# An encoder block's first stage as one explicit list of small operations

## The chip, the cores and the metric

The kernel runs on one core of one Trainium2 chip. The core has five engines with instruction queues of their own: TensorE (PE; its weight loads are shown as PEld), VectorE (DVE), ScalarE (ACT), GpSimd (POOL) and SyncE (SP), which here only issues DMA transfers. Each queue runs in order; engines wait for each other through semaphores. The metric is the device time of one execution in microseconds (us), the median of three runs.

## What is computed

One bidirectional encoder layer on 1024 tokens of width 1024, all in float32 at the interface:

```python
u = rms_norm(x, norm1_g)
q, k, v, cb, cc, ch, ga, gb = split(u @ w_in)        # 512 x 6, then 1024 x 2 columns
q, k = rms_norm(q per head, q_norm_g), rms_norm(k per head, k_norm_g)   # 8 heads of 64
y_a = neighbourhood_attention(q, k, v, rpb) @ w_attn_branch
y_b = (cb * conv3(cc * ch)) @ w_conv_branch
x = x + (sigmoid(ga) * y_a + sigmoid(gb) * y_b) @ w_o
x = x + relu(rms_norm(x, norm2_g) @ w_mlp_in) ** 2 @ w_mlp_out
```

The change concerns the part that comes first: the norm of the rows of x, the product for v, sums of normed rows that a later stage uses for the gates ga and gb (the gate forms), and the first four of eight row blocks of the product for q.

## The kernel before, in words

**Precision.** Every matmul operand is held as two float16 halves, a `hi` (the value, scaled by a power of two and rounded) and a `lo` (the remainder). A product is three passes: hi·hi, hi·lo and lo·hi (`PASSES`). ScalarE makes a `hi` with an activation that copies and scales; VectorE makes the `lo` with `scalar_tensor_tensor` (value times scale, minus `hi`). The power of two comes from a bound over all 128 partitions: a per-partition bound is written into one column of the bfloat16 tile `ones`, one matmul of the all-ones block with that column sums it over the partitions in a bank of PSUM (128x1 output), and VectorE reads it back and works out exponents with a handful of 128x1 instructions (`all_sum`, `pow2`, `pow2_half`).

**Row blocks.** The 1024 tokens are 8 blocks of 128 rows. `load_x(b)` brings block b into `xt`. `norm` squares it on ScalarE with an accumulated sum, works out the reciprocal root of the mean in a few 128x1 VectorE steps and a ScalarE square root (`rstd`), and makes `hi` and `lo` in `u16`, which has room for four blocks. Blocks 0, 1 and 2 are transposed into `uT` by TensorE (`ln_trans`: eight 128x128 transposes for each half into a bank of PSUM, copied out by ScalarE and by VectorE); blocks 3 to 7 by a DMA transpose that SP issues (`ln_turn`).

**V.** The weights of v come in two column halves of 256. For row blocks 0 to 2, each half is a group of its own of 24 matmuls of 256 columns (8 slices of the inner dimension by 3 passes); for blocks 3 to 7 both halves are one group of 24 matmuls of 512 columns (`v_unit`). A part of the weights' `lo` is made on POOL, in two steps.

**Gate forms.** `sforms` runs for four pairs of row blocks (n, n + 4): ScalarE scales both blocks of `xt`, POOL makes four sums and differences of 512 columns, ScalarE rounds them to `hi` (128x2048), VectorE makes the `lo`, and SP stores both in the DRAM tile `gs`.

**Q and K.** For each of the 8 row blocks a group of 24 matmuls of 512 columns for q, then 8 more for k. The result is evicted and processed by `qk_vec`: ScalarE copies and squares, VectorE sums per head, the reciprocal root follows, VectorE scales, ScalarE makes `hi`, VectorE makes `lo` into one of two `q16` buffers, and `finish_qk` has SP transpose it by DMA into `QD` or `KD`. `QD` lies where `xt` was, so its first transpose waits for the last reader of `xt`.

**What sets the order.** Instructions are issued by the program order of Python generators. Foreground generators (`fg`: for example `qk_vec`, `sforms`) go on by `step()`, background ones (`bg`: the preparation of weight chunks, `Chunk.prep`, pushed chunk by chunk) by `tick()`; `unit` issues one group of matmuls and then so many steps and ticks. A generator can hold itself back with `apart(mark, n)` until the counter `units[0]` has reached a value; `flush` sets `forced` and runs the background to its end. For the chunks Q, K and C, `Chunk.prep` squares each weight tile on ScalarE, adds the sums up on VectorE, waits, sums over the partitions with the ones matmul, waits for one more unit, reads back, and scales. The waits are these lines:

```python
                yield from apart(units[0], 2 if self.kind in "QC" else 3)
                yield from all_sum(c, b, bank(self.bank) if self.bank else anybank(), 1e-36)
```

The chunk K is pushed in front of Q's first unit, and the last Q unit is followed by `flush()`. Weight tiles come through a pool of five raw buffers; a tile's load is issued when an earlier tile has been split (`load_upto(done[0] + 5)`).

Of the kernel before, what the change touches and what calls it, by code (L numbers as in the profile page):

```python
# [28 lines left out]
def plan():  # L29


    def block(w, groups, per=2, tiles=8, first=0):
        return [(w, first + k, per, groups) for k in range(0, tiles, per)]

    p = [(("V", j), block("w_in", [(1024 + 256 * j, 256)], 4)) for j in range(2)]
    p += [(("Q", 0), block("w_in", [(0, 512)])), (("K", 0), block("w_in", [(512, 512)]))]
    p += [(("C", j), block("w_in", [(c + 128 * j, 128) for c in (2048, 2560, 1536)])) for j in range(4)]
    branch = lambda j: [((k, j), block(w, [(256 * j, 256)], 4, 4)) for k, w in (("A", "w_a"), ("B", "w_b"))]
    for n in range(8):
        p.append((("S" if n else "G", n), block("w_in", [(3072 + 128 * n, 128), (4096 + 128 * n, 128)], 4)))  # L40
# [30 lines left out]
def encoder_block(ctx: ExitStack, tc: tile.TileContext, x, weights, cols, gqk, rel, masks, out):  # L71
# [16 lines left out]
    def bank16(tag):  # L88
        return psum.tile([128, 1024], F16, name="ps16_" + tag, tag=tag, bufs=banks[tag])
# [23 lines left out]
    def tmp(n=1):  # L113
        return cols_of("tmp", n)
# [267 lines left out]
    def load_x(b):  # L382
        SP.dma_start(xt[:, b], x[b * 128:(b + 1) * 128, :])
# [18 lines left out]
    idi = w1p.tile([128, 128], I32, name="idi", bufs=1)  # L402
    ident = w1p.tile([128, 128], F16, name="ident", bufs=1)
# [43 lines left out]
    def norm(xin, sq, u, y):  # L447

        ss = tmp()
        A.activation(sq, xin, AF.Square, accum_out=sc[:, ss])  # L450
        yield
        yield from rstd(ss, D, y, 9)
        A.activation(u[:, 0], xin, AF.Copy, scale=sc[:, y])
        yield
        V.scalar_tensor_tensor(u[:, 1], xin, sc[:, y], u[:, 0], op0=OP.mult, op1=OP.subtract)

    def ln_trans(u16, b, dst):
        for s in range(2):
            pt = bank16("o")
            for k in range(8):  # L460
                T.transpose(pt[:, k * 128:(k + 1) * 128], u16[:, s, k * 128:(k + 1) * 128], ident)
            o = dst[:, s, :, b * 128:(b + 1) * 128]
            i = pt.rearrange("p (k t) -> p k t", k=8)
            if s == 0:
                A.activation(o, i, AF.Copy)
            else:
                V.tensor_copy(o, i)

    def ln_turn(u16, b, dst):
        SP.dma_start_transpose(dst[:, :, :, b * 128:(b + 1) * 128].rearrange("p s k t -> p (s k) t"),  # L470
                               u16.rearrange("p s k -> p (s k)"))
# [19 lines left out]
    sgq, isgq = keep(), keep()  # L491
    sq = w1p.tile([128, D], F32, name="sq", bufs=1)
    ys = keep(8)
    ln = [norm(xt[:, b], sq, u16[:, b % 4], at(ys, b)) for b in range(8)]
    GS = dram.tile([128, 4, 4, 2, 512], F16, name="gs")

    turned, formed = [0], [0]
    SFORM = (6, 8, 10, 12)

    def sforms():  # L500

        for n, start in enumerate(SFORM):
            yield from apart(start, 0)
            assert turned[0] >= n + 5
            z = []
            for b in (n, n + 4):
                A.activation(xt[:, b], xt[:, b], AF.Copy, scale=sc[:, at(ys, b)])
                z += [xt[:, b, :512], xt[:, b, 512:]]
            f = wqk.tile([128, 4, 512], F32, name="sform", bufs=1)
            v = wqk.tile([128, 4, 2, 512], F16, name="s16", bufs=2)  # L510
            for o, a, b, op in ((2, z[0], z[2], OP.subtract), (0, z[2], z[3], OP.subtract),
                                (1, f[:, 0], z[0], OP.subtract), (3, z[1], f[:, 1], OP.add)):
                G.tensor_tensor(f[:, o], a, b, op=op)
            yield from apart(start, 2)
            A.activation(v[:, :, 0], f, AF.Copy)
            yield
            V.tensor_tensor(v[:, :, 1], f, v[:, :, 0], op=OP.subtract)
            fg.append(sform_store(n, v))

    def sform_store(n, v):  # L520
        yield from apart(units[0], 1)
        SP.dma_start(GS[:, n], v)
        formed[0] = n + 1

    def ln_step(b, n=1):
        for _ in range(n):
            advance(ln[b])
# [7 lines left out]
    def v_unit(b, j, steps, ticks):  # L535
        ps = bank("ds"[b % 2])
        n, c = (512, 0) if j is None else (256, 256 * j)

        def post():
            hi, lo = (VT[:, b, s, c:c + n] for s in range(2))  # L540
            A.activation(hi, ps[:, :n], AF.Copy, scale=2.0 ** -20)
            V.scalar_tensor_tensor(lo, ps[:, :n], 2.0 ** -20, hi, op0=OP.mult, op1=OP.subtract)
        w = vhome[0] if j is None else vhome[0][:, j]
        unit(group(ps[:, :n], [(UT[:, sa, k, b * 128:(b + 1) * 128], w[..., sw, k * 256:(k + 1) * 256])
                               for k in range(8) for sa, sw in PASSES]), post, steps, ticks)

    push(cV[0])
    ln_step(0, 2)
    tick()
    ln_step(0, 5)  # L550
    ln_step(1)
    tick(3)
    ln_step(0)
    ln_step(1)
    tick(4)
    ln_trans(u16[:, 0], 0, UT)
    flush()
    ln_step(1, 5)
    ln_step(1)
    ln_step(2, 2)  # L560
    push(cV[1])
    tick(1)
    v_unit(0, 0, 0, 0)
    ln_step(2, 4)
    ln_trans(u16[:, 1], 1, UT)
    ln_step(2, 1)
    tick(3)
    ln_step(2)
    tick(4)
    ln_step(3, 2)  # L570
    ln_trans(u16[:, 2], 2, UT)
    ln_step(3, 4)
    fg.append(qk_gain())
    fg.append(sforms())
    V.tensor_reduce(sc[:, gm2], sc[:, g1], axis=AX, op=OP.max, apply_absolute_value=True)
    mul(gm2, gm2, gm2)
    for p in range(11):
        if p == 3:
            flush()
            push(cQ)  # L580
        if 0 < p < 6:
            v_unit(p % 3, p // 3, 1, 2)
        elif p:
            v_unit(p - 3, None, 2, 4)
        for q in (p,) if p < 6 else (2 * p - 6, 2 * p - 5):
            c = q // 2 + 3
            if c < 8 and q % 2 == 0:
                ln_step(c, 2)
                ln_turn(u16[:, c % 4], c, UT)
                turned[0] = c + 1  # L590
            if c < 7:
                ln_step(c + 1, 3)
    settle()
    flush()
# [41 lines left out]
    def finish_qk(n):  # L636
# [3 lines left out]
        dst = QD.rearrange("p a e w t -> p (a e w) t") if kind == "q" else KD  # L640
        SP.dma_start_transpose(dst[:, :, b * 128:(b + 1) * 128], q16.pop(n)[0].rearrange("p h w r d -> p (h w r d)"))

    for n, (kind, b) in enumerate(todo):
        ch = cQ if kind == "q" else cK
        if b == 0:
            push(cK if kind == "q" else cConv[0])
        ps = bank("do"[n % 2])
        q16[n] = []

        def post(ps=ps, kind=kind, n=n, ch=ch):  # L650
            fg.append(qk_vec(ps, ch.inv, kind, q16[n]))
        unit(tok_mms(ps, actU, b, ch, 8, 512, 0), post, 4, 3)
        if n == 3:
            forced[0] = True
            while formed[0] < 4:
# [1218 lines left out]
```

## Time and profile before

| what | us |
|---|---|
| median of 3 runs | 1238.45 (1238.36 to 1238.69) |
| profiled execution | 1236.77 |
| its span | 1235.0 |
| TensorE busy in the span | 1196.9 (97%) |
| VectorE / ScalarE / POOL busy | 936.9 / 765.9 / 430.3 |
| start of the first matmul | 9.49 |
| start of the first K group | 114.30 |

How to read the profile: the page gives busy times and shares. The timeline has one row for each instruction or for a few alike in a row: its start and its length in us, engine, line of the kernel, operation, output tile, input tiles, shape, count; in brackets the idle time of the engine before it and the instruction that ended it. The length of a matmul row contains a modelled end; from one group's start to the next is the better measure. All vector and scalar instructions have the line of the recording helper, L66, so they are told apart by their tiles: `u` is a row block's halves, `w_v` V's weight halves, `w_ws` those of Q, K and the later chunks, `s` a gate form's halves, `q` a Q block's halves, `sc` the small columns. The windows view has for each stretch the busy time of PE, PEld, DVE, ACT and POOL with instruction counts, then the clock granted to TensorE as a share, the DMA share and GB/s. The groups view has the count, the sum of busy us and the mean in ns. The DMA view has KB and the median us from issue to landing.

### The profile page before, as it was taken

What the parts mean: (1) busy time and instruction counts of PE and PEld (TensorE: products, weight loads), DVE (VectorE), ACT (ScalarE), POOL (GpSimd) and SP (SyncE); (2) the same over time, 40 slices, a digit from 0 to 9 for tenths busy, and PEclk for the clock granted to TensorE, in tenths of its full rate; (3) what the DMA queues carried; (4) which work ended last, traced back from release to release, by engine and by line L of the source; (5) the groups of instructions that cost most, each with busy time, mean ns of one, the idle gap of its engine ahead of it and who ended that gap; (6) DMA issues with size and microseconds to landing.
All of it is one profiled execution on the core that took longest, in us unless ns stands there. A gap on an engine that the chain in (4) does not pass through costs nothing.

```text
span 1235.0 us, 16691 instructions
## 1 busy us (share of the span) xinstructions
PE 1196.9 (97%) x6102; PEld 576.9 (47%) x6102; DVE 936.9 (76%) x1747; ACT 765.9 (62%) x1185; POOL 430.3 (35%) x289
## 2 busy tenths in 40 slices
PE   5989999999899999999999999999999999999998
PEld 3534445555444444444458444444444444444444
DVE  6668778888558786877878664555547999999997
ACT  6777667768644454535768777777775763646430
POOL 2440003232212111101003466655648373463562
PEclk8999999999899999999999999999999999999999
DMA  6558455565761211216096653454474844435202
GB/s 258 107 200 178 103 118 112 116 153 105 131 154 34 69 52 51 69 35 255 18 174 152 205 170 137 162 187 142 140 290 162 313 155 159 168 116 222 103 35 103
DMA packets 170867, 173.34 MB, mean 140 GB/s; under 512 B 131488, under 2 KB 132000, under 8 KB 166688
## 3 DMA queue, kind: packets, MB, share of 16 engines
q1 hardware_dynamic: 170784, 172.27, 47.2%
q8 instruction: 48, 0.79, 0.3%
q14 instruction: 35, 0.29, 0.1%
HBM read 102.51 MB, written 37.75 MB: 114 GB/s over the span
## 4 chain that ended last, share of the span: by engine, by line
PE 40%; DVE 6%; ACT 2%; issue 2%; DMA 1%; DVEq 0%; ACTq 0%
PE ps_d L207 16%; PE ps_s L207 14%; PE ps_o L207 10%; DVE as L66 1%; DVE ops L66 1%; DVE w L66 1%; DVE form L66 1%; ACT as L66 1%; DVE v L66 1%; DMA u2T<-v 1%; DMA u2x<-v 1%; ACT ops L66 1%; DVE x L66 0%; DVE sc L66 0%; ACT u2x L66 0%
## 5 line engine op out<-in xcount | busy, mean ns | idle before, releaser
L207 PEld LDWEIGHTS <-ops 128*128 128x128 f16 x1356 | 132.4, 98 | 159.9 <-issue 2.7
L207 PEld LDWEIGHTS <-w 128*128 128x128 f16 x1368 | 132.8, 98 | 143.5 <-issue 3.8
L924 PE MATMUL ps_d<-uT,w_ws 128*128 128x512 f16 x576 | 136.7, 382 | 0.0
L207 PE MATMUL ps_s<-ops 128*128 128x512 f16 (+1 forms) x528 | 118.3, 374 | 0.0
L207 PE MATMUL ps_d<-ops 128*128 128x512 f16 x504 | 115.6, 379 | 0.0
L66 ACT ACTIVATE ops<-hf,sc 128x2048 f16<-128x2048 f32 x26 | 52.0, 1999 | 94.0 <-PE ps_d L207 52.7
L207 PE MATMUL ps_d<-u2T,w 128*128 128x512 f16 (+1 forms) x504 | 110.3, 371 | 0.0
L1074 POOL TENSOR_TENSOR tsum<-raw 128x512 f32<-128x512 f32 x28 | 46.6, 1677 | 148.1 <-ACT raw L66 148.1
L207 PEld LDWEIGHTS <-uT 128*128 128x128 f16 x648 | 64.9, 101 | 70.5 <-issue 5.6
L1278 POOL TENSOR_TENSOR as<-as 128x512 f32<-128x512 f32 x56 | 76.7, 1370 | 41.4 <-ACT as L66 38.1
L207 PEld LDWEIGHTS <-w_s 128*128 128x128 f16 x588 | 56.9, 98 | 68.6 <-DVE w_s L66 0.6
L924 PEld LDWEIGHTS <-w_ws 128*128 128x128 f16 x576 | 56.1, 98 | 59.7 <-issue 2.0
L207 PE MATMUL ps_s<-u2x,w 128*128 128x512 f16 (+1 forms) x348 | 78.6, 375 | 0.0
L207 PE MATMUL ps_o<-ops 128*128 128x512 f16 x324 | 74.3, 379 | 2.4 <-DVE as L66 2.4
L66 DVE SCALAR_TENSOR_TENSOR ops<-hf,sc,ops 128x2048 f16<-128x2048 f32 x26 | 71.7, 2759 | 5.7 <-ACT ops L66 5.7
L66 ACT ACTIVATE raw<-raw,sc 128x256 f32<-128x256 f32 x172 | 71.1, 494 | 6.7 <-DMA raw<-in_weights 6.7
L66 DVE TENSOR_TENSOR as<-ps_s,as 128x512 f32<-128x512 f32 (+1 forms) x38 | 23.4, 616 | 58.5 <-ACT as L66 57.9
L66 DVE TENSOR_SCALAR sc<-sc 128x1 int32<-128x1 int32 (+3 forms) x380 | 57.6, 167 | 12.9 <-ACT sq L66 4.3
L1074 POOL TENSOR_TENSOR gsum<-raw 128x512 f32<-128x512 f32 x14 | 18.5, 1340 | 136.8 <-issue 52.3
L66 ACT ACTIVATE w<-raw,sc 128x512 f16<-128x512 f32 (+1 forms) x29 | 25.4, 920 | 50.8 <-DVE sc L66 50.8
L66 ACT ACTIVATE sz<-sz,sc 128x384 f32<-128x384 f32 (+1 forms) x64 | 37.2, 581 | 26.8 <-DVE sc L66 26.6
L66 DVE SCALAR_TENSOR_TENSOR w_ws<-raw,sc,w_ws 128x512 f16<-128x512 f32 (+2 forms) x72 | 48.5, 712 | 6.7 <-ACT w_ws L66 6.7
(261 smaller groups left out, 2548.6 us busy)
## 6 DMA issues: line engine op xcount, KB each, us to landing
raw<-in_weights SPq DMA_DIRECT2D x89, 512.0 KB, 5.5
hs<-as SPq DMA_DIRECT2D x16, 1792.0 KB, 8.7
hf<-hs SPq DMA_DIRECT2D x26, 1024.0 KB, 6.7
w2x<-in_weights SPq DMA_DIRECT2D x16, 512.0 KB, 8.3
raw<-in_weights SPq DMA_DIRECT2D x16, 384.0 KB, 3.7
xt<-in_x SPq DMA_DIRECT2D x8, 512.0 KB, 9.8
gs<-s SPq DMA_DIRECT2D x4, 1024.0 KB, 6.4
x<-in_x SPq DMA_DIRECT2D x8, 512.0 KB, 10.0
```

Source lines behind the costliest of these rows:

```text
L66: return f(out, *a, **kw)
L207: T.matmul(ps, l, r, start=a, stop=b)
L924: T.matmul(ps, l, r, start=a, stop=b)
L1074: G.tensor_tensor(t[:, o], a, b, op=OP.add)
L1278: sub.tensor_tensor(z[o], z[a], z[b], op=op)
```

## The change

The generators `norm`, `ln_trans`, `ln_turn`, `sforms`, `sform_store` and `v_unit`, and the loop that stepped them, are removed. In their place stands one string, `BEGIN`, of words such as `V.1.0.hh.0`; a table `DO` maps a word's first part to a small function, and a loop calls them in the string's order. So each engine's queue is the string's order, projected on that engine. From the fifth Q unit on the old loop goes on, with four ticks instead of three beside each of the last four Q units.

The words: `sq`, `ts`, `sqrt`, `y` are the steps of a row block's norm; `hi` (on POOL for seven blocks, on ScalarE for block 5), `lo`; `Th`, `Tl` the TensorE transposes of blocks 0 to 2, `ch`, `cl` their copies; `turn` a DMA transpose; `tr`, `col`, `one`, `scal` the scale of V's weights, `whi`, `wlo` their halves by 512 columns; `V.b.h.pass.k` four matmuls of one pass; `vh`, `vl` the eviction of V; `zs`, `sp`, `sh`, `sl`, `st` a gate form's scaling, POOL sums, `hi`, `lo` and store; `qs` to `qlo` the same for Q's weights, `Q.b.r` six matmuls, `qc` to `ql` the steps of `qk_vec` for the block, `ldQ`, `ldK` a weight load, and `ks` one square of K's weights (the first also pushes the chunk K).

```diff
+BEGIN = """
+    gm2 sq.0 ts.0 tr.0 sqrt.0 y.0 tr.1 col.0 hi.0.P sq.1 lo.0 Th.0 sq.2 ts.1 one.0 sqrt.1 scal.0 ts.2 ch.0.A
+    Tl.0 sqrt.2 whi.0.1 y.1 whi.0.0 V.0.0.hh.0 whi.1.1 whi.1.0 y.2 hi.1.P Th.1 cl.0.V lo.1 Tl.1 wlo.0.1.P
...
+    hi.6.P V.1.1.hl.1 V.3..hl.0 ldQ.3 V.3..hl.1 vh.3. turn.4 vl.2.0 hi.7.P V.4..hh.0 V.4..hh.1 zs.5
+    V.4..lh.0 qs.1 sl.0 st.0 V.4..lh.1 vh.2.1 vh.1.1 lo.6 qs.0 V.4..hl.0 turn.5 V.4..hl.1 V.5..hh.0
+    V.5..hh.1 V.5..lh.0 turn.6 lo.7 gain qs.3 vl.0.1 vl.1.1 vl.2.1 V.5..lh.1 V.5..hl.0 V.5..hl.1 turn.7 qs.2
...
+    vh.6. zs.7 sh.2 sl.2 st.2 V.7..hl.0 V.7..hl.1 Q.0.0 Q.0.1 Q.0.2 Q.0.3 ldK.0 vl.4. zs.3 Q.1.0 ldK.2 vl.6.
+    Q.1.1 Q.1.2 qc.0 ks.0 Q.1.3 ks.1 Q.2.0 ldK.3 Q.2.1 Q.2.2 Q.2.3 qr.0 qc.1 qr.1 qc.2 qq.0 vh.7. vl.7. qy.0
+    sp.3 ks.2 ks.3 qh.0 Q.3.0 ql.0 sh.3 Q.3.1 sl.3 st.3 Q.3.2 Q.3.3
+"""
...
     load_x(1)
+    load_x(2)
     load_upto(4)
-    load_x(2)
     load_x(3)
+    load_x(4)
+    load_x(5)
     load_upto(5)
+    load_x(6)
+    load_x(7)
...
-    for b in range(4, 8):
-        load_x(b)
...
+    def rows_hi(b, e):
+        o, y = u16[:, b % 4, 0], sc[:, at(ys, b)]
+        if e:
+            G.tensor_scalar(o, xt[:, b], y, 1.0, op0=OP.mult, op1=OP.mult)
+        else:
+            A.activation(o, xt[:, b], AF.Copy, scale=y)
...
+    def v_mms(b, h, kind, kh):
+        g = vgroups.index((b, h))
+        if (kind, kh) == ("hh", 0):
+            vbank[g] = bank("ds"[g % 2])
+        ps = vbank[g][:, :512 if h is None else 256]
+        sa, sw = {"hh": (0, 0), "lh": (1, 0), "hl": (0, 1)}[kind]
+        for k in range(4 * kh, 4 * kh + 4):
+            w = vw[:, :, sw, k * 256:(k + 1) * 256] if h is None else vw[:, h, sw, k * 256:(k + 1) * 256]
+            T.matmul(ps, UT[:, sa, k, b * 128:(b + 1) * 128], w, start=(kind, k) == ("hh", 0),
+                     stop=(kind, k) == ("hl", 7))
...
+    def q_mms(b, r):
+        if r == 0:
+            vbank["q", b] = bank("ds"[(len(vgroups) + b) % 2])
+        for k in (2 * r, 2 * r + 1):
+            for n, (sa, sw) in enumerate(PASSES):
+                T.matmul(vbank["q", b], UT[:, sa, k, b * 128:(b + 1) * 128], cQ.parts[:, sw, 512 * k:512 * k + 512],
+                         start=(k, n) == (0, 0), stop=(k, n) == (7, 2))
+        units[0] += r == 3
...
+          "st": lambda n: SP.dma_start(GS[:, n], sf[n, 1]), "ks": lambda r: (r == 0 and push(cK), tick(1))}
+
+    for word in BEGIN.split():
+        name, *args = word.split(".")
+        DO[name](*[None if name in ("V", "vh", "vl") and a == "" else int(a) if a.isdigit() else a for a in args])
+
+    for b in range(4):
+        q_vec(b, 0)
+        fg.append(qv[b])
...
-        if b == 0:
-            push(cK if kind == "q" else cConv[0])
-        ps = bank("do"[n % 2])
-        q16[n] = []
-
-        def post(ps=ps, kind=kind, n=n, ch=ch):
-            fg.append(qk_vec(ps, ch.inv, kind, q16[n]))
-        unit(tok_mms(ps, actU, b, ch, 8, 512, 0), post, 4, 3)
-        if n == 3:
-            forced[0] = True
-            while formed[0] < 4:
-                step()
-            forced[0] = False
+        if kind == "k" and b == 0:
+            push(cConv[0])
+        if n == 4:
...
-        if n >= 3:
+        if n >= 4:
+            ps = bank("do"[n % 2])
+            q16[n] = []
+
+            def post(ps=ps, kind=kind, n=n, ch=ch):
+                fg.append(qk_vec(ps, ch.inv, kind, q16[n]))
+            unit(tok_mms(ps, actU, b, ch, 8, 512, 0), post, 4, 4 if n < 8 else 3)
             finish_qk(n - 3)
```

More of the change, by code (lines that the diff above doesn't have):

```diff
@@ L445, in pow2_half @@
         yield
[L447 to L471, printed above, removed]
     PASSES = ((0, 0), (0, 1), (1, 0))
@@ L533, in qk_gain @@
         yield from gain(g, 11, sgq, isgq)
[L535 to L594, printed above, removed]
     def bias_load(p):
@@ new lines, in rows_hi, with rows_lo, rows_trans @@
+    def rows_hi(b, e):
[4 more added lines that the diff above has]
+            A.activation(o, xt[:, b], AF.Copy, scale=y)
+    def rows_lo(b):
+        V.scalar_tensor_tensor(u16[:, b % 4, 1], xt[:, b], sc[:, at(ys, b)], u16[:, b % 4, 0],
+                               op0=OP.mult, op1=OP.subtract)
+    pt = {}
+    def rows_trans(b, s):
+        pt[b, s] = bank16("o")
+        for k in range(8):
+            T.transpose(pt[b, s][:, k * 128:(k + 1) * 128], u16[:, b % 4, s, k * 128:(k + 1) * 128], ident)
@@ new lines, in v_col, with w_sum, v_scale @@
+    def v_col(h):
+        m = tmp()
+        mul(g1, rv[h], rv[h])
+        V.tensor_reduce(sc[:, m], sc[:, rv[h]], axis=AX, op=OP.max, apply_absolute_value=True)
+        wcol[h] = ones_col()
+        V.tensor_copy(wcol[h], sc[:, m])
+    def w_sum(h):
+        wbank[h] = bank("o")
+        T.matmul(wbank[h][:, 0:1], ones[:, 0:128], wcol[h], start=True, stop=True)
+    def v_scale(h):
+        b, s = tmp(), tmp()
+        cV[h].inv = keep()
+        V.tensor_scalar(sc[:, b], wbank[h][:, 0:1], 1e-30, None, op0=OP.max)
+        for _ in pow2(b, 14, s, cV[h].inv, False, more=9):
+            pass
+        V.tensor_scalar(sc[:, rv[h]], sc[:, g1], sc[:, s], None, op0=OP.mult)
@@ new lines, in v_out, with q_square @@
+    def v_out(b, h, s):
+        ps = vbank[vgroups.index((b, h))][:, :512 if h is None else 256]
+        hi, lo = (VT[:, b, i, (h or 0) * 256:(h or 0) * 256 + (512 if h is None else 256)] for i in range(2))
+        if s == 0:
+            A.activation(hi, ps, AF.Copy, scale=2.0 ** -20)
+        else:
+            V.scalar_tensor_tensor(lo, ps, 2.0 ** -20, hi, op0=OP.mult, op1=OP.subtract)
+    def q_square(r):
+        A.activation(cQ.parts[:, 1, :1024].bitcast(BF16), cQ.raw[r], AF.Square, accum_out=sc[:, at(rq, r)])
@@ new lines, in q_part @@
+    def q_part(r, i, s):
+        k = 2 * r + i
+        hi, lo = (cQ.parts[:, w, 512 * k:512 * k + 512] for w in range(2))
+        x, c = cQ.raw[r][:, 512 * i:512 * i + 512], sc[:, at(wscale["q"], k)]
+        if s == 0:
+            A.activation(hi, x, AF.Copy, scale=c)
+        else:
+            V.scalar_tensor_tensor(lo, x, c, hi, op0=OP.mult, op1=OP.subtract)
+            w_did(("q", r))
+    def q_mms(b, r):
[6 more added lines that the diff above has]
+        units[0] += r == 3
@@ new lines, in encoder_block, with q_vec, s_scaled, s_sums @@
+    qv = {}
+    def q_vec(b, n):
+        if b not in qv:
+            q16[b] = []
+            qv[b] = qk_vec(vbank["q", b], cQ.inv, "q", q16[b])
+        for _ in range(n):
+            advance(qv[b])
+    def s_scaled(b):
+        A.activation(xt[:, b], xt[:, b], AF.Copy, scale=sc[:, at(ys, b)])
+    def s_sums(n):
+        z = [xt[:, b, 512 * i:512 * i + 512] for b in (n, n + 4) for i in range(2)]
+        f = sf[n] = wqk.tile([128, 4, 512], F32, name="sform", bufs=1)
+        for o, a, b, op in ((2, z[0], z[2], OP.subtract), (0, z[2], z[3], OP.subtract),
+                            (1, f[:, 0], z[0], OP.subtract), (3, z[1], f[:, 1], OP.add)):
+            G.tensor_tensor(f[:, o], a, b, op=op)
@@ L665, in encoder_block @@
             mk = wbias.tile([128, 2, 384], BF16, name="mk", bufs=1)
-            SP.dma_start(mk, masks)
             cneg, cinv = keep(), keep()
```

132 lines of the change are left out of this document (104 added, 28 removed).

## The prediction

> **What bounds the kernel now.** I read the page first, then TensorE's timeline up to the K projection, then VectorE, ScalarE and the DMA issues beside it. Names: V.b is the V product of row block b, Q.b and K.b the query and key products; `hi` and `lo` are the two float16 halves of an operand.
>
> ```profile
> span 1235.0 us, 16691 instructions
> PE 1196.9 (97%) x6102; PEld 576.9 (47%) x6102; DVE 936.9 (76%) x1747; ACT 765.9 (62%) x1185; POOL 430.3 (35%) x289
> ```
>
> TensorE is busy for 97% of the span, so a change here is worth what it does to TensorE's gaps, and to its clock.
>
> ```profile
> 13.04 5.13 PE L207 MATMUL ps_d<-w_v,uT 128*128 128x256 f16 x23 [0.34 <-DVE w_v L66]
> 23.48 0.18 PE L198 MATMUL ps_o<-ones 128*128 128x1 bf16 x1 [3.53 <-DVE ones L66]
> ...
> 25.57 4.36 PE L207 MATMUL ps_s<-w_v,uT 128*128 128x256 f16 x24
> ...
> 35.66 2.78 PE L207 MATMUL ps_s<-w_v,uT 128*128 128x256 f16 x24
> 38.27 2.78 PE L207 MATMUL ps_d<-w_v,uT 128*128 128x256 f16 x24
> ...
> 46.07 5.34 PE L207 MATMUL ps_d<-w_v,uT 128*128 128x512 f16 x24
> ...
> 51.28 5.34 PE L207 MATMUL ps_s<-w_v,uT 128*128 128x512 f16 x24
> ...
> 64.15 5.35 PE L207 MATMUL ps_s<-w_v,uT 128*128 128x512 f16 x24 [2.35 <-DMA uT<-u]
> 69.34 0.38 PE L207 MATMUL ps_d<-w_ws,uT 128*128 128x512 f16 x1
> ...
> 74.94 3.24 PE L207 MATMUL ps_d<-w_ws,uT 128*128 128x512 f16 x14 [0.87 <-DVE w_ws L66]
> 78.02 5.34 PE L207 MATMUL ps_o<-w_ws,uT 128*128 128x512 f16 x24
> ...
> 98.74 0.17 PE L198 MATMUL ps_s<-ones 128*128 128x1 bf16 x1
> ...
> 109.12 5.34 PE L207 MATMUL ps_o<-w_ws,uT 128*128 128x512 f16 x24
> 114.30 1.89 PE L207 MATMUL ps_d<-w_ws,uT 128*128 128x512 f16 x8
> ```
>
> The reader sees V.4 at 46.07, V.5 at 51.28, V.7 after 2.35 us of waiting for its transposed row block, Q.0 drawn out to 8.68 us (69.34 to 78.02) because its weight halves are late, and Q.7 from 109.12, with K.0 behind it at 114.30 and no gap. A full group of 512 columns takes 5.18 (114.30 - 109.12), one of 256 columns 2.61 (38.27 - 35.66). The matmul at 98.74 is the sum for K's weight scale, three Q units ahead of K.0: that distance is what the change alters most. From K.0 on, the two kernels have the same instructions in the same order on every engine, so I measure by the start and the pace of K.0 and carry the difference to the end.
>
> ```profile
> 22.00:24.00 2.00, 0.52 (x6) 0.52 (x7) 1.90 (x5) 1.33 (x3) 0.00 (x0) 0.50 0.60 240
> 28.00:30.00 2.00, 2.00 (x17) 1.63 (x16) 1.17 (x1) 1.84 (x3) 0.00 (x0) 0.80 0.02 4
> ```
>
> The third figure from the end is the granted clock: half after the 3.53 us gap, and in part of 28 to 30 still. So 24 matmuls took 4.36 at 25.57 instead of 2.61. From 23.5 to about 28.6 is 5.1 us at half clock, which lost about 2.5 us.
>
> **The change, part by part: Begin.** Its matmuls are the same: three row blocks are transposed on TensorE before and after. What goes is the 3.53 us gap and the half clock behind it (2.5): passes over V's first weight half fill that place. What comes: the first product needs four `hi` pieces instead of one, about 1 us; the second half's `lo` on VectorE now run beside POOL's gate sums.
>
> ```profile
> 47.00 2.51 POOL L513 TENSOR_TENSOR sform<-xt 128x512 f32<-128x512 f32 x2 [11.62 <-ACT xt L66]
> 48.27 2.32 DVE L66 SCALAR_TENSOR_TENSOR u<-xt,sc,u 128x1024 f16<-128x1024 f32 x1 [0.61 <-ACT u L66]
> ```
>
> Beside POOL that `lo` took 2.32; it waits out one POOL operation of 1.26 (2.51 / 2). I take one such wait, 1.3. V.4 would then start 3.5 + 2.5 - 1.0 - 1.3 = 3.7 us early, at about 42.4. This lead does not last, and V.5 decides why. SP's queue runs in order, and in the changed order the store of the first gate form stands in front of the transpose of row block 5. The store waits for that form's `lo` on VectorE.
>
> ```profile
> L66 DVE SCALAR_TENSOR_TENSOR u<-xt,sc,u 128x1024 f16<-128x1024 f32 x7 | 10.0, 1432 | 6.2 <-ACT u L66 6.2
> ...
> L66 DVE TENSOR_REDUCE sc<-raw 128x4 f32<-128x1024 f32 x4 | 4.9, 1214 | 0.0
> L66 DVE SCALAR_TENSOR_TENSOR w_v<-raw,sc,w_v 128x256 f16<-128x256 f32 x8 | 4.1, 575 | 0.0
> ```
> ```profile
> 0.00:50.00 50.00, 34.90 (x237) 24.60 (x238) 33.03 (x92) 36.45 (x67) 12.77 (x24) 0.93 0.66 212
> ```
> ```profile
> gs<-s SPq DMA_DIRECT2D x4, 1024.0 KB, 6.4
> ...
> uT<-u SPq DMA_TRANSPOSE x5, 4.3
> ```
> ```profile
> 88.02 2.29 DVE L66 TENSOR_TENSOR s<-sform,s 128x2048 f16<-128x2048 f32 x1 [2.33 <-ACT s L66]
> ...
> 90.31 0.68 DVE L66 TENSOR_REDUCE sc<-sq 128x8 f32<-128x512 f32 x1
> ...
> 99.72 0.15 DVE L66 TENSOR_SCALAR sc<-ps_s 128x1 f32<-128x1 f32 x1
> 100.89 1.23 DVE L66 TENSOR_TENSOR q<-qs,q 128x1024 f16<-128x1024 f32 x1 [1.03 <-ACT q L66]
> ...
> 111.35 1.40 DVE L66 SCALAR_TENSOR_TENSOR w_ws<-raw,sc,w_ws 128x512 f16<-128x512 f32 x2
> ...
> 112.82 1.40 DVE L66 SCALAR_TENSOR_TENSOR w_ws<-raw,sc,w_ws 128x512 f16<-128x512 f32 x2
> 114.15 0.68 DVE L66 TENSOR_TENSOR qs<-qs,sc 128x512 f32<-128x512 f32 x1
> 114.75 0.19 DVE L66 RECIPROCAL sc<-sc 128x8 f32<-128x8 f32 x1
> ```
>
> Ahead of that `lo` VectorE has, by the order of instructions, 59 small ones at 0.15, six row-block `lo` at 1.43, four reductions at 1.21, eight weight `lo` at 0.575 and five evictions of about half a us each (estimate, after the 0.575 of the same width): 8.9 + 8.6 + 4.9 + 4.6 + 2.5 = 29.5, from about 4.5 on, then 2.29 itself: it ends at 36 if VectorE never idles. Before, VectorE idled 17 of its first 50 us (33.03 busy), 12.5 of them after 4.5. I take 7.5 us of idling: 44. Store and transpose are issued by 44.6; alone the transpose lands 4.3 later, a store takes 6.4, so behind one I take 6.4: V.5 starts at 51, as before (51.28), after TensorE has idled 3 to 5 us. The half clock then costs 2.5 again: V.6 at 58.7, V.7 at 63.9, Q.0 at 69.1. With its halves ready, Q.0 takes 5.18 and perhaps 0.5 of waiting, instead of 8.68: **3.2 us gained**, and Q.7 ends at 111.1. Bounds: 10.7 gained if V.5 does not wait at all (5 and 2.5 more), 3 lost if VectorE idles 6 us more.
>
> **K's scale.** The generator that prepares K's weights waits for three more units after its squares. Before, the squares were through at Q.1, and the sum stood behind Q.4. In the changed order they are only through at Q.4, so the sum stands behind Q.7, directly in front of K.0, and the flush behind it emits the rest. Nothing covers that chain. On VectorE the read-back of the sum stands behind all vector steps of Q.4, most of Q.5's, and Q.6's reduction and reciprocal. Before, Q.6's reciprocal came at 114.75, behind four `lo` of K (2.8 by the rows at 111.35 and 112.82) that will not be there: 111.95, or 2.3 before Q.7's end. But VectorE enters the Q phase later. In the new list the last gate form's `lo` stands, through ScalarE, behind Q.2's eviction and everything listed after it.
>
> ```profile
> 79.31 1.04 ACT L66 ACTIVATE w_ws<-raw 128x1024 bf16<-128x1024 f32 x1
> ...
> 86.08 1.91 ACT L66 ACTIVATE s<-sform 128x2048 f16<-128x2048 f32 x1 [1.41 <-DMA gs<-s]
> 87.90 0.67 ACT L66 ACTIVATE qs<-ps_o,sc 128x512 f32<-128x512 f32 x1
> 88.60 0.63 ACT L66 ACTIVATE sq<-qs 128x512 f32<-128x512 f32 x1
> ```
> ```profile
> 110.58 2.54 ACT L66 ACTIVATE w_ws<-raw,sc 128x512 f16<-128x512 f32 x4
> ...
> 115.58 1.04 ACT L66 ACTIVATE q<-qs 128x1024 f16<-128x1024 f32 x1
> ```
>
> From Q.2's end: eviction 0.67, square 0.63, two squares of K at 1.04, Q.0's `hi` 1.04, the form's `hi` 1.91, its `lo` 2.29: 8.6, with two short ScalarE steps 9. Before, this `lo` ended at 90.31, 1.9 after Q.2's end (83.20 plus 5.18). The lag grows by 7.1, and the read-back falls 7.1 - 2.3 = 4.8 after Q.7's end. From there: nine small steps at 0.15, one Q `lo` 1.23 and one scaling 0.68 on VectorE, then Q.6's `hi` 1.04 and K's first `hi` 0.64 (2.54 / 4) on ScalarE: 4.9. K.0 starts 9.7 after Q.7's end; bounds 5.1 (no lag: 0.17 for the sum and the 4.9) and 12 (the two Q buffers also wait for their transposes). After that gap K.0 runs at half clock: 2.5, bounds 0 and 5. **K.0 costs 12.2.** Its `lo` come at 0.70 each (1.40 / 2) against 0.65 of TensorE per slice, which hides them. The conv weights' loads move behind K's flush, five in a row; K.0 to K.3, 20.7 us, cover them (bound 3).
>
> **Sum.** -3.2 + 12.2 = +9.0. The profiled execution took 1236.77 (span 1235.0), 1.7 under the median of the three runs, 1238.45; against the median the forecast is **1247.4**.
>
> [...]
>
> **Rivals.**
> - VectorE has caught up by Q.7: K.0 waits 5.1, plus 2.5, less 3.2: +4.4, **1242.9**. For it: by the rhythm of before the read-back would find its place free. Against: the 9 us chain after Q.2. Chance 0.20.
> - VectorE and POOL get in each other's way more: single-input POOL operations hold VectorE's two-input ones too, and five of the row-block `hi` on POOL cost one POOL operation each, 1.26 as above, before V.5: +6, **1253.5**. For it: the 2.32 row. Against: only two-input POOL work stands beside it there. Chance 0.13. [...]
> - Faster: VectorE idles little in Begin. It decides if the first form's `lo` ends by 40: V.5 then starts without a wait, Begin gains 10.7, VectorE enters the Q phase without the lag, and K.0 costs 5.1 + 2.5: -3.1, **1235.3**. For it: 36 is possible by the sum. Against: 17 us idle of 50 before. Chance 0.10.
> - The change does nothing to the time: gain and K.0's cost meet near 7.5, 1238.4. Chance 0.03.
>
> **How the numbers follow.** The forecast has 0.54. Within 0.2% (2.5 us) is about what a measurement of this kernel can tell from no change. Faster 0.10, same 0.03, slower 0.87 by these cases. The range 1241 to 1256 takes in the forecast with its bounds, the caught-up VectorE and the busier POOL, and leaves out the faster case.
>
> **What would show it.** Right: a gap of 8 to 12 us on TensorE in front of K.0, ended by a ScalarE `hi` of K's weights; half clock in K.0; a gap of 3 to 5 us in front of V.5, ended by a transpose; no waits on VectorE in Q.0. Wrong: K.0 within 6 us of Q.7, or V.5 without a gap.

## Result, and the profile after

| | kernel before | changed kernel |
|---|---|---|
| median, first runs (4 each) | 1238.40 us (1236.12 to 1238.69) | 1253.63 us (1252.96 to 1254.16) |
| ratio to before | | 1.0127, 95% interval 1.0109 to 1.0144 |
| median, later runs on one chip | 1240.05 us | 1252.84 us, ratio 1.0101 (1.0084 to 1.0119) |
| profiled execution, its span | 1236.77, 1235.0 us | 1253.64, 1251.9 us |
| first matmul | 9.49 | 10.30 |
| Q.0 starts | 69.34 | 72.76 |
| Q.7 ends | 114.30 | 114.54 |
| K.0 starts | 114.30 | 126.03 |
| K.1 starts | 119.48 | 134.38 |

The change made the kernel slower by 15.2 us (medians of the first runs; 12.8 by the later ones); the forecast was +9.0. The first median lies 6.2 us above the forecast, inside the range. Both places at which the prediction saw the loss are there, and both cost more than forecast.

The changed kernel's page, its span and busy times:

```profile
span 1251.9 us, 16697 instructions
PE 1202.5 (96%) x6102; PEld 577.7 (46%) x6102; DVE 943.2 (75%) x1746; ACT 759.3 (61%) x1179; POOL 442.1 (35%) x296
```

Its TensorE timeline from V.4 to K.1, to be held against the one of the kernel before:

```profile
43.23 5.34 PE L665 MATMUL ps_s<-w_v,uT 128*128 128x512 f16 x24
54.57 7.97 PE L665 MATMUL ps_d<-w_v,uT 128*128 128x512 f16 x24 [5.99 <-DMA uT<-u]
62.38 1.03 PE L665 MATMUL ps_s<-w_v,uT 128*128 128x512 f16 x4
...
72.76 2.97 PE L708 MATMUL ps_s<-w_ws,uT 128*128 128x512 f16 x13
75.91 2.54 PE L708 MATMUL ps_s<-w_ws,uT 128*128 128x512 f16 x11 [0.18 <-DVE w_ws L89]
78.28 5.34 PE L708 MATMUL ps_d<-w_ws,uT 128*128 128x512 f16 x24
83.46 5.34 PE L708 MATMUL ps_s<-w_ws,uT 128*128 128x512 f16 x24
88.64 5.34 PE L708 MATMUL ps_d<-w_ws,uT 128*128 128x512 f16 x24
...
109.36 5.34 PE L230 MATMUL ps_o<-w_ws,uT 128*128 128x512 f16 x24
114.54 0.17 PE L221 MATMUL ps_s<-ones 128*128 128x1 bf16 x1
126.03 0.59 PE L230 MATMUL ps_d<-w_ws,uT 128*128 128x512 f16 x1 [11.31 <-ACT w_ws L89]
127.34 7.21 PE L230 MATMUL ps_d<-w_ws,uT 128*128 128x512 f16 x23 [0.72 <-DVE w_ws L89]
134.38 5.34 PE L230 MATMUL ps_o<-w_ws,uT 128*128 128x512 f16 x24
```

Two stops carry the loss. V.5 waits 5.99 us for its transposed row block and then takes 7.81 (62.38 - 54.57) instead of 5.18. K.0 waits 11.31 us for ScalarE's first `hi` of K's weights, behind the sum at 114.54, and takes 8.35 (134.38 - 126.03). Between them the Q groups run at one per 5.18 us: Begin as a whole came out even (Q.7 ends 0.24 us later than before), and K.0 cost 14.7 (11.5 from Q.7's end to its start, and 3.2 more in itself). Begin's start scatters by a microsecond: in four other traces with the same list up to V.5 (experiments 2, 5, 7 and 10) V.5 starts at 53.61 to 54.13 and Q.7 ends at 113.39 to 114.03, so the trace above is the latest of five.

The windows of the same execution (PE, PEld, VectorE, ScalarE and POOL busy, granted clock, DMA share, GB/s):

```profile
4.50:47.42 42.92, 32.97 (x238) 24.01 (x239) 36.31 (x83) 30.40 (x60) 26.69 (x27) 1.00 0.61 204
...
126.00:131.00 5.00, 4.25 (x10) 1.39 (x10) 5.00 (x8) 4.97 (x9) 0.00 (x0) 0.50 0.34 96
131.00:136.00 5.00, 5.00 (x23) 2.22 (x22) 2.27 (x8) 4.61 (x11) 0.00 (x0) 0.94 0.97 244
```

The first row shows VectorE busy for 36.31 us up to the end of the first gate form's `lo`; the second the half clock in the first 5 us of K.0, the third its return. Why that `lo` and the read-back of K's sum came late shows on VectorE's, POOL's, SP's and ScalarE's timelines of the changed kernel:

```profile
13.83 0.90 DVE L89 TENSOR_TENSOR sc<-sc 128x1 f32<-128x1 f32 x1
...
41.27 2.12 DVE L89 SCALAR_TENSOR_TENSOR u<-xt,sc,u 128x1024 f16<-128x1024 f32 x1 [0.23 <-ACT u L89]
...
44.30 3.10 DVE L89 TENSOR_TENSOR s<-sform,s 128x2048 f16<-128x2048 f32 x1
...
120.95 0.11 DVE L89 TENSOR_SCALAR sc<-ps_s 128x1 f32<-128x1 f32 x1
```
```profile
13.61 1.12 POOL L579 TENSOR_SCALAR u<-xt,sc 128x1024 f16<-128x1024 f32 x1 [3.37 <-DVE sc L89]
```
```profile
47.42 0.35 SPq L754 DMA_DIRECT2D gs<-s  x1
47.82 9.52 SPq L602 DMA_TRANSPOSE uT<-u  x3
```
```profile
105.10 1.06 ACT L89 ACTIVATE q<-qs 128x1024 f16<-128x1024 f32 x1 [1.95 <-DVE qs L89]
110.56 1.06 ACT L89 ACTIVATE q<-qs 128x1024 f16<-128x1024 f32 x1 [4.41 <-DMA qD<-q]
```

A VectorE operation on one column took 0.90 us instead of 0.16 and ended at 14.73, when POOL's `hi` ended (13.61 + 1.12). Row block 5's `lo`, the row at 41.27, was done at 43.39. The form's `lo` took 3.10 instead of the 2.29 of before and ended at 47.40; SP issued the store at 47.42 and the transpose for V.5 behind it, at 47.82. Later ScalarE stood still for 4.41 us because the fourth Q block's `hi` (the row at 110.56) found both `q` buffers waiting for their transposes; VectorE's read-back of K's sum came at 120.95, 6.4 us after Q.7's end.

### The profile page after: what moved, and what is told of

It reads as the page before. It is cut to its first block, busy times and chain, and to the rows that moved or that the text cites. A ratio compares the mean times of both kernels' runs of the same rounds, so it can differ in the third digit from the quotient of the medians.

```text
span 1251.9 us, 16697 instructions
## 1 busy us (share of the span) xinstructions
PE 1202.5 (96%) x6102; PEld 577.7 (46%) x6102; DVE 943.2 (75%) x1746; ACT 759.3 (61%) x1179; POOL 442.1 (35%) x296
## 4 chain that ended last, share of the span: by engine, by line
PE 41%; DVE 6%; ACT 2%; issue 2%; DMA 1%; DVEq 0%; ACTq 0%
PE ps_d L230 16%; PE ps_s L230 14%; PE ps_o L230 11%; DVE as L89 1%; DVE ops L89 1%; DVE w L89 1%; DVE form L89 1%; DVE v L89 1%; DMA u2x<-v 1%; DMA u2T<-v 1%; ACT ops L89 1%; ACT as L89 0%; DVE x L89 0%; DVE sc L89 0%; ACT u2x L89 0%
## 5 line engine op out<-in xcount | busy, mean ns | idle before, releaser
L1192 POOL TENSOR_TENSOR tsum<-raw 128x512 f32<-128x512 f32 x28 | 46.4, 1672 | 150.1 <-ACT raw L89 150.1
L89 ACT ACTIVATE w_ws<-raw,sc 128x512 f16<-128x512 f32 (+2 forms) x72 | 41.3, 637 | 18.9 <-DVE sc L89 18.9
```

Source lines behind the costliest of these rows:

```text
L89: return f(out, *a, **kw)
L1192: G.tensor_tensor(t[:, o], a, b, op=OP.add)
```

## The experiments

Each is compared by its ratio to the kernel before, run beside it, and by where K.1 starts in its trace. K.1 is the first point behind both stops, and what comes later has the same instructions in all of them (119.48 before; 134.38 in the changed kernel, 133.23 when it was run again, so a difference of about 1 us in K.1 is scatter).

### 1. The first gate form's store behind the transposes

```diff
-    V.4..lh.0 qs.1 sl.0 st.0 V.4..lh.1 ... turn.5 ... turn.6 ... turn.7 qs.2
+    V.4..lh.0 qs.1 sl.0 V.4..lh.1 ... turn.5 ... turn.6 ... turn.7 st.0 qs.2
```

> Changed kernel with one move: the store of the first gate form stands behind the transpose of row block 7 instead of in front of that of block 5. Theory (SP's queue): V.5 loses its wait of 5.99 and most of the half clock behind it (V.5 took 7.8 instead of 5.18, 2.6), so Q.7 ends 7 to 8.6 us earlier, near 106.5, and the time falls to 1245 to 1247. Rival (the row halves themselves are late on VectorE, and the queue is no matter): V.5 or V.6 keeps a wait of 3 us or more, and the time stays above 1250. K.0's wait of 11.3 stays in both.

Measured: 1244.58 us, ratio 1.0045 (1.0028 to 1.0063); K.1 at 126.36. TensorE's timeline of this kernel:

```profile
42.83 5.34 PE L665 MATMUL ps_s<-w_v,uT 128*128 128x512 f16 x24
48.01 5.34 PE L665 MATMUL ps_d<-w_v,uT 128*128 128x512 f16 x24
53.19 1.03 PE L665 MATMUL ps_s<-w_v,uT 128*128 128x512 f16 x4
...
117.23 0.59 PE L230 MATMUL ps_d<-w_ws,uT 128*128 128x512 f16 x1 [11.01 <-ACT w_ws L89]
```

V.5 starts at 48.01 without a stop and takes 5.18 (53.19 - 48.01) instead of 7.81; K.0's wait stays. SP issues the transpose for V.5 at 43.02 instead of 47.82. So the one word `st.0` in front of `turn.5` cost the 8.0 us at K.1 (6.9 against the second run of the changed kernel): the data of V.5's transpose had been ready, and only SP's queue held it. The time came out just under the expected 1245.

### 2. K's sum behind Q.4

```diff
-                yield from apart(units[0], 2 if self.kind in "QC" else 3)
+                yield from apart(units[0], 2 if self.kind in "QC" else 0 if self.kind == "K" else 3)
```

> Changed kernel with one move: the sum for K's weight scale stands behind Q.4, where the kernel before has it, instead of behind Q.7. Theory (the exposed chain): K.0's wait of 11.3 falls under 4 and its half clock (8.35 instead of 5.18) mostly goes; 8 to 14 us less, 1240 to 1246. Rival (VectorE and ScalarE are late in the whole Q phase, wherever the sum stands): the sum itself or K.0 still waits 6 us or more, and the time stays above 1247.

Measured: 1245.87 us, ratio 1.0054 (1.0034 to 1.0074); K.1 at 125.16, 9.2 us earlier than in the changed kernel. TensorE's timeline:

```profile
98.30 0.16 PE L221 MATMUL ps_s<-ones 128*128 128x1 bf16 x1
...
116.09 0.38 PE L230 MATMUL ps_d<-w_ws,uT 128*128 128x512 f16 x1 [2.06 <-ACT w_ws L89]
116.88 4.22 PE L230 MATMUL ps_d<-w_ws,uT 128*128 128x512 f16 x12 [0.41 <-DVE w_ws L89]
122.59 2.73 PE L230 MATMUL ps_d<-w_ws,uT 128*128 128x512 f16 x11 [1.50 <-DVE w_ws L89]
```

The sum's place makes most of K.0's wait, as the theory has it, but not all: even with the sum 15.7 us ahead of Q.7's end, K.0 stops for 4.0 us in three places (2.06, 0.41, 1.50). Something else was late on VectorE and ScalarE; experiments 5 and 8 look for it.

### 3. Both moves

```diff
-    V.4..lh.0 qs.1 sl.0 st.0 V.4..lh.1 ... turn.7 qs.2
+    V.4..lh.0 qs.1 sl.0 V.4..lh.1 ... turn.7 st.0 qs.2
...
+                yield from apart(units[0], 2 if self.kind in "QC" else 0 if self.kind == "K" else 3)
```

> Both moves at once (the first gate form's store behind the transpose of block 7, K's sum behind Q.4). If the two costs are apart: the sum of the two gains, 15 to 22 us under the changed kernel, 1232 to 1239, at or under the kernel before. If an earlier V.5 only makes the Q phase run into the late VectorE: the second gain shrinks by what the first one won, and the time stays at 1241 or more.

Measured: 1236.97 us, ratio 0.9983 (0.9968 to 0.9998); K.1 at 118.46. The moves took 8.0 and 9.2 us off K.1 one by one, and 15.9 together: within the scatter of about 1 us the two costs are independent. By the interval this kernel stands level with the one before or just under it.

### 4. The kernel before, with its sum behind Q.7

```diff
-                yield from apart(units[0], 2 if self.kind in "QC" else 3)
+                yield from apart(units[0], 2 if self.kind in "QC" else 6 if self.kind == "K" else 3)
```

> Kernel before, with one move the other way: K's sum stands behind Q.7 instead of behind Q.4. It prices the exposed chain alone, without the changed order's late VectorE. If the prediction's split holds: a wait of about 5.1 in front of K.0 and 2.5 of half clock, +7.6, 1246. If the lag is no part of it and the place of the sum alone makes the whole: a wait near 11 and +14.7, 1253. If VectorE's and ScalarE's work of Q.4 to Q.6 covers it: under +3.

Measured: 1245.66 us, ratio 1.0055 (1.0034 to 1.0077); K.1 at 126.46, 7.0 later than before. TensorE's timeline:

```profile
114.36 0.17 PE L198 MATMUL ps_s<-ones 128*128 128x1 bf16 x1
118.84 0.38 PE L207 MATMUL ps_d<-w_ws,uT 128*128 128x512 f16 x1 [4.32 <-ACT w_ws L66]
120.15 6.47 PE L207 MATMUL ps_d<-w_ws,uT 128*128 128x512 f16 x23 [0.93 <-DVE w_ws L66]
126.46 5.34 PE L207 MATMUL ps_o<-w_ws,uT 128*128 128x512 f16 x24
```

This is the price of the exposed chain alone: 4.5 us from the sum to K.0, and K.0 slower by 2.4 (7.62 instead of 5.18). Of the 11.5 us between the changed kernel's sum and K.0, 7.0 are then of another origin.

### 5. Four buffers for the halves of a Q block

```diff
-        t = wqk.tile([128, 8, 2, r, HD], F16, name=kind + "16", tag="q16")
+        t = wqk.tile([128, 8, 2, r, HD], F16, name=kind + "16", tag="q16", bufs=4)
...
-        sf[n, 1] = wqk.tile([128, 4, 2, 512], F16, name="s16", bufs=2)
+        sf[n, 1] = wqk.tile([128, 4, 2, 512], F16, name="s16", bufs=1)
```

> Changed kernel with four instead of two buffers for the halves of a Q or K block (and one instead of two for the halves of a gate form, to make room). It asks what makes the read-back of K's sum fall 6.4 us after Q.7's end. Theory (ScalarE stands still for 4.41 us at 106 to 110.5 because the fourth block's halves wait for the transpose of the second, which stands on SP's queue behind the fourth gate form's store, the mask and the bias): that wait goes, the read-back falls about 2 us after Q.7's end, K.0's wait of 11.3 shrinks to about 7, the time falls by 4 to 5, 1249. Rival (the 9 us of work behind Q.2 on VectorE and ScalarE alone, as the prediction has it): another wait takes its place, K.0's wait stays above 10 and the time within 2 us of the changed kernel.

Measured: 1248.36 us, ratio 1.0065 (1.0041 to 1.0089); K.1 at 128.55. TensorE's and VectorE's timelines:

```profile
113.39 0.17 PE L221 MATMUL ps_s<-ones 128*128 128x1 bf16 x1
119.39 0.59 PE L230 MATMUL ps_d<-w_ws,uT 128*128 128x512 f16 x1 [5.84 <-ACT w_ws L89]
```
```profile
114.31 0.10 DVE L89 TENSOR_SCALAR sc<-ps_s 128x1 f32<-128x1 f32 x1
```

The read-back falls 0.9 us after Q.7's end (114.31 - 113.39) instead of 6.4, and K.0's wait is 5.84 instead of 11.31: from the sum to K.0 pass 6.0 us instead of 11.5. Nothing of the order changed, and the last form's `lo` still ends 9.5 us behind Q.2's end (97.00 - 87.49). So the lag of the read-back was made by two buffers and the transposes that empty them, not by the work listed behind Q.2. Whether the transposes' place on SP's queue, behind a store and two loads, makes them late was not tried by itself. The wait fell by more than expected (5.84 for about 7).

### 6. GpSimd's operations of Begin narrowed

```diff
-            G.tensor_scalar(o, xt[:, b], y, 1.0, op0=OP.mult, op1=OP.mult)
+            G.tensor_scalar(o[:, :8], xt[:, b, :8], y, 1.0, op0=OP.mult, op1=OP.mult)
```

and the same for the two operations of V's weight `lo` on POOL. The kernel leaves out most columns of these halves, which are filled with zeros once at the start.

> Changed kernel in which GpSimd's operations of Begin on row halves and on V's weight halves work on 8 columns instead of 1024 or 256 (the rest of these halves is left zero, so the output is not the reference's); VectorE's and ScalarE's work is the same. Theory (GpSimd holds VectorE's operations up): VectorE's row `lo` fall from 1.68 to about 1.3, its weight `lo` from 0.95 to about 0.45, the first gate form's `lo` ends some 4 us earlier (43 to 44 instead of 47.4), V.5 waits 2 us less and starts at 50 to 52, and the time falls 3 to 5, 1249 to 1250. Rival (VectorE is late because of its own work and waits, and the two do not hold each other up): the durations and the end of the form's `lo` stay within 1 us, and so does the time.

Measured: 1247.18 us, ratio 1.0059 (1.0036 to 1.0083); K.1 at 128.38. TensorE's and VectorE's timelines:

```profile
49.59 7.04 PE L667 MATMUL ps_d<-w_v,uT 128*128 128x512 f16 x24 [3.77 <-DMA uT<-u]
```
```profile
40.13 2.29 DVE L89 TENSOR_TENSOR s<-sform,s 128x2048 f16<-128x2048 f32 x1 [0.56 <-ACT s L89]
```

The form's `lo` takes 2.29 again and ends at 42.42, 5.0 us earlier, and V.5 starts 5.0 us earlier (49.59 instead of 54.57; 4.0 to 4.5 against the four other traces with this list). By the groups of the first 50 us a row `lo` on VectorE takes 1.41 us instead of 1.68, a weight `lo` 0.69 instead of 0.95. A rival would be that POOL's own `hi` are through sooner and VectorE waits less for them. The windows from the first row `lo` to the end of the form's `lo` settle it: the same 72 VectorE instructions were busy for 32.49 us of 36.70 in the changed kernel (10.70 to 47.40) and for 26.73 of 30.67 here (11.75 to 42.42). Of the 6.0 us, 5.8 are shorter operations and 0.3 less idling. GpSimd holding VectorE up made these 5 us. V.5 and the time moved a little further than expected (50 to 52, 1249 to 1250 us), the single operations less far (1.3 and 0.45 expected).

### 7. TensorE kept busy in front of K.0

```diff
             ps = bank("do"[n % 2])
+            for _ in range(48 if n == 8 else 0):
+                T.matmul(ps, actU(0, 0)[:, :128], actU(0, 0)[:, :512], start=True, stop=True)
```

> Changed kernel with 48 matmuls of 512 columns, whose result is not used, between Q.7 and K.0, in place of TensorE's wait there (10.4 us of 11.3). It prices the half clock behind the wait alone. Theory (TensorE's clock falls because it stood idle): K.0's first matmul starts when it did, and K.0 takes 5.2 to 6 instead of 8.35, 2.5 to 3.2 less, 1250.5 to 1251. Rival (K.0 is slow because its weights' halves come late, not by the clock): K.0 still takes 7.5 or more and nothing is gained.

Measured: 1250.16 us, ratio 1.0080 (1.0058 to 1.0103). TensorE's timeline:

```profile
124.79 0.38 PE L230 MATMUL ps_d<-w_ws,uT 128*128 128x512 f16 x1 [0.86 <-ACT w_ws L89]
126.10 5.23 PE L230 MATMUL ps_d<-w_ws,uT 128*128 128x512 f16 x23 [0.93 <-DVE w_ws L89]
131.17 5.34 PE L230 MATMUL ps_o<-w_ws,uT 128*128 128x512 f16 x24
```

K.0 starts 11.4 us after Q.7's end, as in the changed kernel (11.5), and takes 6.38 us (131.17 - 124.79) instead of 8.35: the half clock behind the stop is worth 2.0 by these two traces. K.0 took 8.2 to 9.2 in the five traces with a stop of this kind (the changed kernel's two and experiments 1, 5 and 6), which would make 1.8 to 2.8. The other 1.2 above 5.18 are left: the second matmul waits 0.93 for a `lo`, which the prediction had called hidden. That is why K.0 stayed above the expected 5.2 to 6.

### 8 and 9. Versions meant to beat both

Experiment 8 joins the moves of 1 (store behind the transpose of block 6), 2 and 5. Experiment 9 is the same, with the gate forms' tiles in a region of their own, so that they keep their two buffers. The part of 8 that is new:

```diff
-    V.4..lh.0 qs.1 sl.0 st.0 V.4..lh.1 ... turn.6 lo.7
+    V.4..lh.0 qs.1 sl.0 V.4..lh.1 ... turn.6 st.0 lo.7
```

> A version meant to beat both: changed kernel with the first gate form's store behind the transpose of row block 6, K's sum behind Q.4, and four buffers for Q's halves (one for the gate form's). If the residue in front of K.0 (2.8 us in the kernel with the first two moves, and half clock behind it) comes from ScalarE's waits for the transposes of Q's halves, 3.5 us each: 2 to 4 us under that kernel, 1233 to 1235. If it comes from the order of VectorE's work: 1236 to 1238, as that kernel.

Measured: 1236.12 us, ratio 0.9968 (0.9952 to 0.9984); K.1 at 114.89. TensorE's timeline in Q.0:

```profile
68.35 4.22 PE L708 MATMUL ps_s<-w_ws,uT 128*128 128x512 f16 x11 [2.01 <-DVE w_ws L89]
```

The time fell into the range of the rival, but the stop in front of K.0 (2.78 us in experiment 3) is gone, as the theory has it. What ate the gain is new: Q.0 now waits 2.01 us for a weight `lo`, and the 11 matmuls behind that take 4.22 instead of the changed kernel's 2.54.

```diff
+    psf = ExitStack()
+    wsf = psf.enter_context(tc.tile_pool(name="psf", bufs=2, side="right"))
...
-        sf[n, 1] = wqk.tile([128, 4, 2, 512], F16, name="s16", bufs=2)
+        sf[n, 1] = wsf.tile([128, 4, 2, 512], F16, name="s16", bufs=2)
...
             pln.close()
+            psf.close()
```

> The combined version again, with the gate forms' tiles in a region of their own that is given back before the masks come, so that Q's halves have four buffers and the gate form's halves keep their two. In the combined version Q.0 waited 2.01 us for a weight `lo` and then ran at half clock (11 matmuls in 4.22 instead of 2.5). If that came from the gate form's single buffer: Q.0's wait falls to about 0.6, no half clock behind it, 3 us less, 1232 to 1234 and 0.4 to 0.6% under the kernel before. If VectorE's order makes it: Q.0 keeps a wait of 1.5 or more, and the time stays at 1236.

Measured: **1232.97 us, ratio 0.9943 (0.9928 to 0.9958)**, 0.6% faster than the kernel before and the fastest of all; K.1 at 112.58, 6.9 earlier than before. TensorE's timeline around K.0:

```profile
101.47 5.34 PE L230 MATMUL ps_o<-w_ws,uT 128*128 128x512 f16 x24
106.66 2.97 PE L230 MATMUL ps_d<-w_ws,uT 128*128 128x512 f16 x13
110.01 2.73 PE L230 MATMUL ps_d<-w_ws,uT 128*128 128x512 f16 x11 [0.39 <-DVE w_ws L89]
112.58 5.34 PE L230 MATMUL ps_o<-w_ws,uT 128*128 128x512 f16 x24
```

Q.0's wait is 0.64, so the single gate-form buffer had made the 2.01. With three details put right (a store in front of a transpose, a late sum, two buffers) the explicit order of Begin is worth 7 us; in the changed kernel they took 20 us away (1252.84 - 1232.97). The kernel before was not run with four buffers, but its timeline has no stop between Q.1 and K.1 that they could remove.

### 10. The changed kernel again

> The changed kernel as it is, beside the others on the same chip. If the profiled execution of the changed kernel had bad luck with the clock behind the two stops of 2.4 us near 721 and 964 us (12 matmuls in 4.14 and 4.44 instead of 2.75), its runs scatter by up to 3.4 us and the two stops are followed by full clock in some of them; the ratio to the kernel before stays within 1.011 to 1.0144. If the clock there belongs to the changed order, both stops are followed by half clock again.

Measured: 1252.84 us, ratio 1.0101 (1.0084 to 1.0119). Behind both stops of 2.4 us far behind the change 12 matmuls took 2.75 this time, yet the profiled execution (1252.85) was only 0.8 us shorter: in the attention stage it waited longer for a transpose instead (one wait of 4.28). The first half of the expectation's bet holds, that the slow matmuls behind those stops do not belong to the changed order; the bound on the ratio missed at its lower end, 1.0101 for 1.011.

## Why the prediction was right, and where it was not

**Direction and places: right.** A stop in front of V.5 ended by a transpose, a stop of 8 to 12 us in front of K.0 ended by ScalarE's `hi`, half clock behind both (0.50 granted from 54.57 to 59.00 and from 126.03 to 131.00), Q.0 drawn together: all are in the trace. Experiments 1, 2 and 3 show that the store in front of the transpose and the place of K's sum cause them.

**V.4 3.7 us early, at 42.4: nearly.** 43.23, 2.8 early.

**The form's `lo` ends at 44: wrong, 47.4** (46.4 to 47.4 over all traces with this list but experiment 6's). This is the first mis-sized term. The prediction took one hold of 1.3 by POOL and 7.5 of idling. The idling was 6.6 (42.92 - 36.31), but VectorE was busy for 36.31 us instead of 31.8. The prediction priced a row `lo` at 1.43 and a weight `lo` at 0.575; beside POOL's new work they took:

```profile
L89 DVE SCALAR_TENSOR_TENSOR u<-xt,sc,u 128x1024 f16<-128x1024 f32 x8 | 13.3, 1684 | 0.6 <-issue 0.3 <-ACT u L89 0.2
L89 DVE SCALAR_TENSOR_TENSOR w_v<-raw,sc,w_v 128x256 f16<-128x256 f32 x8 | 7.2, 945 | 0.0
```

**V.5 at 51 after 3 to 5 us, half clock 2.5: late by the same.** 54.57 after 5.99; the half clock 2.6 (7.81 - 5.18). **Q.0 in 5.7: right,** 5.52. So **Begin's gain of 3.2 was not there** (0.24 lost): 3.4 of the miss; in the changed kernel's second trace 0.7 was gained, and 2.5 missed.

**The read-back 4.8 us after Q.7's end: 6.4, and for another reason.** The chain behind Q.2's end was forecast at 9 and was 9.5 (the last form's `lo` ended at 98.15, Q.2 at 88.64). But experiment 5 leaves that chain alone, and the read-back falls at 0.9. The step that failed is that this lag lasts until the read-back: VectorE caught up, and then the halves of Q's blocks, with two buffers and a transpose queue behind a store, held ScalarE for 4.41. The prediction named that only as a bound.

**From the read-back to K.0 4.9: right,** 5.1. **Half clock in K.0 2.5: 2.0** (experiment 7; 1.8 to 2.8 over five traces). **"Its `lo` hide": wrong, 1.2.** Together K.0 cost 14.7 instead of 12.2, 2.5 of the miss. **The conv weights' loads are covered: right;** K.1 to K.3 have no stop.

**The rest of the span.** Up to K.1 the loss was 14.9 against 9.0: 3.4 and 2.5 are the whole miss there. The spans differ by 16.9. The 2.0 beyond lie within the scatter of what comes after K.1: that stretch took 1114.7 to 1120.4 us in the twelve traces, 1115.5 before and 1117.5 in the changed kernel; nothing shows that they belong to the change.

**The rivals.** "VectorE has caught up by Q.7" did not come, but experiment 4 is its case: the rival priced it at 5.1 and 2.5, and 4.5 and 2.4 were measured. The faster rival did not come either. It counts a wait of 5 us for V.5, where the prediction's own times (V.4 from 42.4, V.5 at 51) leave 3.4; so its 10.7 should be 9.1. Experiment 1 takes V.5's wait away by another way: there Q.7 ended 8.2 us earlier than before (106.06), but K.0's stop stayed at 11.0. "VectorE and POOL get in each other's way more" gave 1253.5, and 1253.63 came; its mechanism is shown by experiment 6, which took 5.0 us off V.5 and 6.0 off K.1 (4.9 against the second run of the changed kernel). Its number fits so well partly by chance, since 2.5 of the miss lie at K.0, and the later runs give +12.8, not +15. The prediction spoke against it with "only two-input POOL work stands beside it there". That holds for the row it looked at, but the trace of before has single-input POOL work elsewhere, and it holds VectorE's two-input operations there:

```profile
25.57 1.85 POOL L310 TENSOR_SCALAR scaled<-raw,sc 128x256 f32<-128x256 f32 x4 [8.82 <-issue]
```
```profile
26.61 0.36 DVE L66 SCALAR_TENSOR_TENSOR sc<-sc 128x1 f32<-128x1 f32 x1
27.00 0.42 DVE L66 TENSOR_TENSOR sc<-sc 128x1 f32<-128x1 f32 x1
```

Such an operation takes 0.16 where POOL stands still, and the second of them ended at 27.42, with POOL's row. So this rival's mechanism could have been read from the trace of before. The changed kernel's trace shows the same: the one-column operation of 0.90 us that ended with POOL's `hi`.

**The clock.** The prediction took 2.5 us for a stop's half clock, from the row at 25.57 and the windows beside it (5.1 us at half clock). Behind V.5's stop of 6 us 2.1 to 2.6 were lost in five traces, behind K.0's 1.8 to 2.8: around the row's price. The sum is hardly touched by it.

## What to carry to other kernels

In a list of operations ordered for one engine, look at each queue that the list shares: a store that waits for late data in front of a transpose whose data is ready cost 7 to 8 us here, and moving one word gave them back. The scale that is summed over the partitions had a chain of 4.5 us behind the sum in experiment 4, and of 5.1 behind its read-back in the changed kernel; with the sum three units of 5.18 us ahead of its use, as in the kernel before and in experiment 9, it was covered, but count the buffers that the work in between needs. When work moves to GpSimd, look at VectorE's two-input operations beside it, also where the GpSimd work has a single input: here one of 0.16 us took 0.90 beside such a row, and 11.4 us less of GpSimd's work (25.57 busy against 14.17 in the windows of experiment 6) gave VectorE 5.8 us back.

## What was not expected of the hardware

The same stop costs TensorE's clock or does not. Far behind the change both kernels stop for 2.38 us in front of the same group, here in the timelines of the kernel before and of the changed kernel:

```profile
948.51 2.75 PE L207 MATMUL ps_o<-ops 128*128 128x512 f16 x12 [2.38 <-DVE as L66]
```
```profile
963.70 4.44 PE L230 MATMUL ps_o<-ops 128*128 128x512 f16 x12 [2.38 <-DVE as L89]
```

Behind it 12 matmuls took 2.75 us in the one, at a granted clock of 1.00, and 4.44 in the other, at 0.59: 1.7 more. Two such stops of 2.4 us stand in each of the twelve traces; nine of the 24 were followed by slow matmuls, 12 of which took 4.1 to 4.4 us, and the kernels themselves do not tell which. The changed kernel's first profiled execution had both slow, the one before none, its second execution none. In the first they made 3.4 us (1.7 each, at the one near 721 over two groups of 12), and shorter waits for transposes in the attention stage (4.6 in all, 5.8 before) gave some of it back: together that is about the 2.0 that its span lost behind K.1. In the second execution, which lost 2.3 there, the transposes were waited for longer (7.6 in all). This may be one cause of the scatter of the runs, which is 1 to 8 us for one kernel; only the profiled executions show it. In these traces a stop of 2.4 us was enough for the slow matmuls, though not always. What decides each case was not tried.

One more: in experiment 6 a POOL fill of 8192 columns ran from 1.01 for 6.92 us, to 7.93, and a VectorE operation with one input of 128 columns, which takes 0.23 in the changed kernel, started at 1.10 and ended at 8.01. So single-input VectorE work seems to be held at times too; this is one case, and it was not tried apart.
